# Two of eleven gate/up groups by a seven-product scheme in an fp32 feed-forward kernel

## The chip, the cores and the metric

The kernel runs on one core of a Trainium2 chip. The metric is the time of one execution on the device in microseconds; the time before is the median of three runs, 965.41 us (964.82 to 967.43). The engines of a core work side by side, each through its own list of instructions in order: PE multiplies matrices, DVE works element by element, ACT does activations and casts, POOL small things, and SP issues the DMAs. Semaphores tie them together.

## The reference

Two layers, each with a half-step feed-forward block, a mixer (attention) and a second feed-forward block, on 256 tokens of width 1024:

```
D_MODEL = 1024; SEQ = 256; DEPTH = 2; D_FF = 2816
def swiglu(h, w_gate, w_up, w_down):
    return (jax.nn.silu(h @ w_gate) * (h @ w_up)) @ w_down
...
    for i in range(DEPTH):
        h = rmsnorm(x, ffn1_norm[i])
        x = x + 0.5 * swiglu(h, ffn1_w_gate[i], ffn1_w_up[i], ffn1_w_down[i])
        ...
        h = rmsnorm(x, ffn2_norm[i])
        x = x + 0.5 * swiglu(h, ffn2_w_gate[i], ffn2_w_up[i], ffn2_w_down[i])
```

## The kernel before

All weights are fp32. A product in that precision is made of three matmuls of rounded parts: each operand is split into hi (its value rounded to PE's fp32r) and lo (what the rounding left), and PE adds x_hi·w_hi, x_hi·w_lo and x_lo·w_hi in one bank. That is `dense` (lines 416, 419 and 422): one *dense step* multiplies a 128 x 128 block of x with a 128 x 512 block of weights.

A **gate/up stage** (`gu`; there are four, one for each feed-forward block) computes h @ w_gate and h @ w_up. It takes the 2816 hidden columns in 11 groups of 256 (256 of gate and 256 of up stand side by side, 512 columns), and each group in two **chunks** of 512 rows, 1 MB each. A chunk is loaded by two DMAs, gate and up, into one of three raw buffers (line 281), split by ACT (`hi`, a cast, line 321) and DVE (`lo`, a subtraction, line 340), 512 columns at a time, into one of four hi/lo buffers, and multiplied with both halves of the tokens: 8 dense steps, 24 matmuls. Then `evac` makes h = silu(gate) * up of each token half (ACT `sil`, line 526; DVE `h`, line 529), transposes 32 x 32 blocks (line 537) and turns the rest by way of DRAM (`hd` out, `hr` back), after which h is split in its turn (`ht`, lines 557 and 559, or with small sums for some chunks, lines 573 to 586). The **down** projection follows (`acc`); there, three chunks of the last three stages are already multiplied by a seven-product scheme (`seven`, `m`).

The program writes its own order. A planner (`Flow`) keeps a clock for PE and free times for the other engines while the kernel is being recorded; generators for the loads, casts, residuals and evacuations are resumed as their estimated times come due, and each instruction is recorded in the order in which this happens. So numbers such as `yield flow.now + 4.0` (how long the read of `hr` is thought to take) move instructions and are no waits on the chip. `raw_left` and `hl_left` count the free raw and hi/lo buffers, `banks` the eight PSUM banks, `g2` and `g4` the scratch tiles. On the chip each instruction waits for semaphores, in its engine's order.

## Time and profile before

| | before |
|---|---|
| median of 3 runs | 965.41 us (964.82 to 967.43) |
| the profiled execution | 964.95 us |
| its span, first to last instruction | 963.2 us |
| granted PE clock | 1.000 |
| HBM read | 188.99 MB |

The profile is of one execution. A row of a group gives line, engine, operation, output<-inputs, shape and count, then busy time in total and the mean of one in ns, then the idle time of the engine just before. A row of a timeline gives start and length in us, and in brackets how long the engine had been idle and what ended that. In a table of stretches each engine has its busy time and count, then come the granted clock of PE, the share of the DMA engines and GB/s. PE's records overlap, because matmuls are pipelined: their distance is read from start to start.

### The profile page before, as it was taken

Reading aid. Unit: us, or ns where it says so; the run is one execution under the profiler, and the core shown is the slowest. Engines: PE = TensorE matmul, PEld = TensorE weight load, DVE = VectorE, ACT = ScalarE, POOL = GpSimd, SP = SyncE. Lnnn points to the kernel's source line nnn. Section 1 sums busy time; section 2 is a strip of 40 time slices with the busy share of each in tenths; the row PEclk is TensorE's granted clock in tenths of the full one; section 3 lists DMA queues with packets and bytes.
Section 4 is the critical chain, followed back from the end, with each engine's and each line's share of the span. In section 5 each row is a group of like instructions: output and inputs, shape, how many; then the busy total and the mean of one; then the engine's idle time right before and its main releaser. Section 6 shows DMA issues by size and latency. Waiting matters only on the chain.

```text
span 963.2 us, 13464 instructions
## 1 busy us (share of the span) xinstructions
PE 954.8 (99%) x4525; PEld 783.9 (81%) x4525; DVE 745.0 (77%) x1569; ACT 567.9 (59%) x1215; POOL 60.5 (6%) x65
## 2 busy tenths in 40 slices
PE   8999999999999999999999999999999999999998
PEld 7888888888777888888888888888787788888886
DVE  6777777788777877759986775797989886776785
ACT  6655555666676655545645555565677765554551
POOL 0000000021210000000000000000343100000000
PEclk9999999999999999999999999999999999999999
DMA  8988877486525479766568777666641468777661
GB/s 282 328 267 285 250 263 246 145 272 208 176 88 175 154 224 284 235 229 205 184 208 254 247 245 220 212 202 219 207 143 44 134 196 283 232 254 225 215 190 44
DMA packets 169295, 204.04 MB, mean 212 GB/s; under 512 B 9673, under 2 KB 144394, under 8 KB 169226
## 3 DMA queue, kind: packets, MB, share of 16 engines
q1 hardware_dynamic: 169226, 203.18, 66.0%
q8 instruction: 35, 0.57, 0.2%
q14 instruction: 34, 0.28, 0.1%
HBM read 188.99 MB, written 14.16 MB: 211 GB/s over the span
## 4 chain that ended last, share of the span: by engine, by line
PE 94%; DVE 3%; ACT 1%; DMA 1%; SPq 0%; issue 0%; ACTq 0%
PE gu L422 17%; PE gu L416 17%; PE gu L419 17%; PE acc L416 9%; PE acc L422 9%; PE acc L419 9%; PE pj L422 3%; PE pj L416 3%; PE pj L419 3%; PE xtp L429 1%; PE ptp L429 1%; PE S L1139 1%; PE AV L1220 1%; PE m L422 1%; PE m L419 1%; PE m L416 1%
## 5 line engine op out<-in xcount | busy, mean ns | idle before, releaser
L340 DVE TENSOR_TENSOR lo<-raw,hi 128x512 fp32r<-128x512 f32 x647 | 413.7, 684 | 103.9 <-ACT hi L321 100.0
L321 ACT CAST hi<-raw 128x512 fp32r<-128x512 f32 x647 | 361.7, 618 | 219.0 <-PE gu L422 123.6
L422 PE MATMUL gu<-hi,xl 128*128 128x512 f32 x704 | 274.3, 390 | 0.0
L416 PE MATMUL gu<-hi,xh 128*128 128x512 f32 x704 | 274.1, 389 | 0.0
L419 PE MATMUL gu<-lo,xh 128*128 128x512 f32 x704 | 274.0, 389 | 0.0
L422 PEld LDWEIGHTS gu<-hi,xl 128*128 128x128 f32 x704 | 132.2, 188 | 27.4
L419 PEld LDWEIGHTS gu<-lo,xh 128*128 128x128 f32 x704 | 132.2, 188 | 27.3
L416 PEld LDWEIGHTS gu<-hi,xh 128*128 128x128 f32 x704 | 132.2, 188 | 27.3
L416 PE MATMUL acc<-hi,ht 128*128 128x512 f32 x280 | 109.6, 391 | 0.0
L422 PE MATMUL acc<-hi,ht 128*128 128x512 f32 x280 | 109.2, 390 | 0.0
L419 PE MATMUL acc<-lo,ht 128*128 128x512 f32 x280 | 109.1, 390 | 0.0
L422 PE MATMUL pj<-hi,xl 128*128 128x512 f32 x160 | 64.5, 403 | 0.0
L419 PE MATMUL pj<-lo,xh 128*128 128x512 f32 x160 | 63.6, 397 | 0.0
L416 PE MATMUL pj<-hi,xh 128*128 128x512 f32 x160 | 63.5, 397 | 0.0
L422 PEld LDWEIGHTS acc<-hi,ht 128*128 128x128 f32 x280 | 52.6, 188 | 11.0
L419 PEld LDWEIGHTS acc<-lo,ht 128*128 128x128 f32 x280 | 52.6, 188 | 10.7
L416 PEld LDWEIGHTS acc<-hi,ht 128*128 128x128 f32 x280 | 52.6, 188 | 10.7
L526 ACT ACTIVATE sil<-gu,xr 128x256 f32<-128x256 f32 x88 | 41.5, 472 | 28.6 <-PE gu L422 28.6
L559 DVE TENSOR_TENSOR ht<-hr,ht 128x512 fp32r<-128x512 f32 x35 | 24.1, 687 | 32.2 <-ACT ht L557 32.2
L529 DVE SCALAR_TENSOR_TENSOR h<-gu,xr,sil 128x256 f32<-128x256 f32 x88 | 42.2, 479 | 5.8 <-ACT sil L526 4.5
L557 ACT CAST ht<-hr 128x512 fp32r<-128x512 f32 x35 | 21.6, 618 | 41.9 <-DMA hr<-hd 41.8
L436 POOL TENSOR_TENSOR xr<-v,nhalf 128x1 f32<-128x1 f32 x12 | 8.4, 698 | 502.3 <-DVE v L434 502.3
(191 smaller groups left out, 1069.0 us busy)
## 6 DMA issues: line engine op xcount, KB each, us to landing
raw<-in_ffn_w_down_dram SPq DMA_DIRECT2D x176, 256.0 KB, 4.1
raw<-in_ffn_w_gate_dram SPq DMA_DIRECT2D x86, 512.0 KB, 4.3
raw<-in_ffn_w_up_dram SPq DMA_DIRECT2D x86, 512.0 KB, 5.5
raw<-in_w_in_dram SPq DMA_DIRECT2D x32, 512.0 KB, 4.1
hd<-hb SPq DMA_DIRECT2D x44, 256.0 KB, 2.3
hr<-hd SPq DMA_DIRECT2D x44, 256.0 KB, 5.3
raw<-in_w_out_dram SPq DMA_DIRECT2D x8, 1024.0 KB, 5.0
raw<-in_w_mem_kv_dram SPq DMA_DIRECT2D x4, 1024.0 KB, 5.4
```

The source lines that it names most:

```text
L321: nc.scalar.copy(out=c.part(0, q), in_=c.block(q))
L340: nc.vector.tensor_sub(c.part(1, q), c.block(q), c.part(0, q).bitcast(F32))
L416: nc.tensor.matmul(out=ps, lhsT=xh, rhs=wh, start=start, stop=False)
L419: nc.tensor.matmul(out=ps, lhsT=xh, rhs=wl, start=False, stop=False)
L422: nc.tensor.matmul(out=ps, lhsT=xl, rhs=wh, start=False, stop=stop)
L429: nc.tensor.transpose(out=dst, in_=src, identity=flip if flipped else ident)
L526: nc.scalar.activation(sil, ps[tb][:, 0:256], AF.Silu, scale=xt.r[tb])
L529: nc.vector.scalar_tensor_tensor(out=h, in0=ps[tb][:, 256:512], scalar=xt.r[tb], in1=sil, op0=ALU.mult, op1=ALU.mult)
L557: nc.scalar.copy(out=hi, in_=src)
L559: nc.vector.tensor_sub(lo, src, hi.bitcast(F32))
L1139: nc.tensor.matmul(out=ss[e][:, pr, :nk], lhsT=q[rows, pr, :], rhs=k[rows, pr, :], start=i == 0, stop=i == len(passes) - 1)
L1220: nc.tensor.matmul(out=av[64 * e:64 * e + 64, pr, :], lhsT=vsrc(kb, pr, e), rhs=pts[e][:, pr, kb, :], start=(kb == 0), stop=(kb == nb - 1))
```

## The change

In the last three of the four gate/up stages, groups 3 and 4 are computed together. Take the normalised tokens as two halves of 128 (1 and 2) and the 1024 inputs as two halves of 512: X11, X12, X21, X22. Take the weights of both groups as B11, B21 (group 3, the two chunks) and B12, B22 (group 4). Instead of eight products of such blocks there are seven, each of four dense steps:

```
T1 = B12 - B11    T3 = B22 - B12    T2 = B22 - T1    T4 = B21 - T2
F0 = X21 + X22    F2 = X11 - X21    F1 = F0 - X11    F3 = X12 - F1
m1 = X11 B11   m5 = F0 T1   m7 = F2 T3   m6 = F1 T2   m3 = F3 B22   m2 = X12 B21   m4 = X22 T4
group 3: m1 + m2 and m1 + m6 + m7 + m4      group 4: m1 + m6 + m5 + m3 and m1 + m6 + m5 + m7
```

DVE makes the T (`wsum`, line 338 of the changed kernel) from raw weights, 512 columns at a time, and they are split as weights are. The forms F (`y`, `xf`) are made once a stage from the scaled, transposed tokens, which `prep_half` now keeps. The products go to banks of their own (`pair_m`), and DVE adds them up (`pair_sums`, line 770) into scratch tiles, from which `evac` reads. The order of work is products and plain chunks in turn: after group 2, m1, chunk, m5, chunk, m7, chunk, m6, chunk, m3, two chunks, m2, chunk, m4, and the remaining chunks; block 11 is loaded first, then 12, 22 and 21 where the list has them. Raw blocks are held until the last sum that reads them.

Besides, every chunk of gate/up weights but the first two of the program is now split 1024 columns at a time, two casts and two residuals instead of four (blocks that enter products unsummed too); summed blocks and all other weights stay at 512. And the planner counts 6.5 us instead of 4.0 for the read of `hr`.

The diff, cut to its core:

```diff
+    class Item:
+        def __init__(self, raws, uses=8, w=1):
+            self.raws, self.uses = raws, uses
+            self.hi = self.lo = None
+            self.hit, self.lot, self.st = [None] * 7, [None] * 7, [None] * 4
+            self.n, self.frees, self.takes, self.gives = 1, 1, 0, 0
+            self.sums, self.t = [], []
+            self.index = len(items)
+            w = 1 if len(items) < 2 else w
+            self.units = [(self.own(q, w), q, w, None) for q in range(0, 4, w)]
+            items.append(self)
...
+        for i, it in enumerate(items):
+            yield lambda: hl_left[0] >= it.n and all(r.raw is not None for r in it.raws)
+            hl_left[0] -= it.n
+            yield max(r.early or r.arrive for r in it.raws)
+            it.hi, it.lo = ([whl.tile([P, 2048], F32R, tag=x, name=f"{x}{i}_{j}") for j in range(it.n)]
+                            for x in ("hi", "lo"))
+            for src, q, w, dep in it.units:
                 if q == 2:
+                    yield max(r.arrive for r in it.raws)
+                if dep is not None:
+                    yield lambda: it.st[dep] is not None
+                    yield it.st[dep]
                 yield calm_a(i)
+                nc.scalar.copy(out=it.part(0, q, w), in_=src())
+                t = flow.act(512 * w)
+                it.hit[q:q + w] = [t] * w
 
     def split_lo():
+        for i, it in enumerate(items):
+            if it.sums:
+                yield lambda: all(r.raw is not None for r in it.raws) and g2.left >= it.takes + 2
+                yield max(r.arrive for r in it.raws)
+                it.t += [g2.take([P, 512], F32, "wsum") for _ in range(it.takes)]
+                for j, (x, y) in enumerate(it.sums):
                     yield calm_v(i)
+                    nc.vector.tensor_sub(it.t[j], x(), y())
+                    it.st[j] = flow.dve(512)
+            for src, q, w, dep in it.units:
+                yield lambda: it.hit[q] is not None
+                yield it.hit[q]
                 yield calm_v(i)
+                nc.vector.tensor_sub(it.part(1, q, w), src(), it.part(0, q, w).bitcast(F32))
+                t = flow.dve(512 * w)
+                it.lot[q:q + w] = [t] * w
+            raw_left[0] += it.frees
+            g2.give(it.gives)
...
+    PAIR = {(0, 1): None, (0, 2): 3, (1, 1): 3, (1, 2): 3}
...
+    def pair_items(raws):
+        r11, r12, r22, r21 = raws
+        def sums(need, x, y, held=None):
+            it = Item(need, 4)
+            it.t, it.takes = (held.t, 0) if held else ([], 4)
+            at_ = lambda v, j: it.own(j, 1, v) if isinstance(v, int) else (lambda: v.t[j])
+            it.sums = [(at_(x, j), at_(y, j)) for j in range(4)]
+            it.units = [((lambda j=j: it.t[j]), j, 1, j) for j in range(4)]
+            return it
+        def plain(r, frees):
+            it = Item([r], 4, 2)
+            it.frees = frees
+            return it
+        made = {}
+        def m1():
+            made["b11"] = plain(r11, 0)
+        def m5():
+            made["t1"] = sums([r12, r11], 0, 1)
+        def m7():
+            made["t3"] = sums([r22, r12], 0, 1)
+            made["t3"].gives = 4
+        def m6():
+            made["t2"] = sums([r22], 0, made["t1"], made["t1"])
+            made["t2"].frees = 0
+        def m3():
+            made["b22"] = plain(r22, 1)
+        def m2():
+            made["b21"] = plain(r21, 0)
+        def m4():
+            made["t4"] = sums([r21], 0, made["t2"], made["t2"])
+            made["t4"].gives = 4
+        return made, dict(m1=m1, m5=m5, m7=m7, m6=m6, m3=m3, m2=m2, m4=m4)
...
+        gu = {}
+        pair = PAIR[l, nm]
+        work = [(g, c) for g in range(NG) for c in range(2)]
+        if pair is not None:
+            rest = [w for w in work if w[0] not in (pair, pair + 1)]
+            n = 2 * pair
+            p = iter(rest[n:])
+            work = rest[:n]
+            loads = {}
+            for x in ("11", "m1", "p", "12", "m5", "p", "22", "m7", "p", "m6", "p", "m3", "p", "p", "21", "m2", "p", "m4"):
+                work.append(next(p) if x == "p" else x)
+            work += list(p)
+            blocks = {"11": (pair, 0), "12": (pair + 1, 0), "22": (pair + 1, 1), "21": (pair, 1)}
+            raws = [Chunk(parts(*blocks[x])) for x in ("11", "12", "22", "21")]
+            made, mk = pair_items(raws)
+            which = dict(zip(("11", "12", "22", "21"), raws))
+        for w in work:
+            if w in ("11", "12", "22", "21"):
+                chunks.append(which[w])
+            elif isinstance(w, str):
+                mk[w]()
+            else:
+                gu[w] = add_chunk(parts(*w), 8, 2)
...
+        if xt.keep:
+            xt.y[tb, hf] = y
+        else:
+            g2.give()
...
-                banks.give()
+                (gives or (banks, banks))[tb].give()
...
-            yield flow.now + 4.0
+            yield flow.now + 6.5
...
+        def pair_forms():
+            yield lambda: len(xt.y) == 4 and g4.left >= 4
+            y = xt.y
+            fm = [g4.take([P, 2, 4, P], F32R, "xf") for _ in range(4)]
+            for j, op, o, a, b in ((0, nc.vector.tensor_add, (1, 1), (1, 0), (1, 1)),
+                                   (2, nc.vector.tensor_sub, (1, 0), (0, 0), (1, 0)),
+                                   (1, nc.vector.tensor_sub, (0, 0), (1, 1), (0, 0)),
+                                   (3, nc.vector.tensor_sub, (0, 1), (0, 1), (0, 0))):
+                yield lambda: flow.free["V"] <= flow.now + SLACK
+                op(y[o], y[a], y[b])
+                flow.dve(512)
+            for j, o in ((0, (1, 1)), (2, (1, 0)), (1, (0, 0)), (3, (0, 1))):
+                yield lambda: flow.free["A"] <= flow.now + SLACK
+                nc.scalar.copy(out=fm[j][:, 0], in_=y[o])
+                yield flow.act(512)
+                yield lambda: flow.free["V"] <= flow.now + SLACK
+                nc.vector.tensor_sub(fm[j][:, 1], y[o], fm[j].bitcast(F32)[:, 0])
+                xt.ft[j] = flow.dve(512)
+                g2.give()
+            xt.fm = fm
+        def pair_sums():
+            def plus(o, x, m):
+                nc.vector.tensor_add(o, x, m)
+                return flow.dve(512)
+            yield lambda: "m1" in mt
+            yield mt["m1"]
+            yield g2.has()
+            u = g2.take([P, 512], F32, "gu_u")
+            nc.scalar.copy(out=u, in_=pb["m1"])
+            yield flow.act(512)
+            banks.give()
+            yield lambda: "m6" in mt and "m7" in mt
+            yield mt["m6"]
+            yield g2.has(3)
+            u2, w, v = (g2.take([P, 512], F32, "gu_v") for _ in range(3))
+            plus(u2, u, pb["m6"])
+            banks.give()
+            plus(w, u2, pb["m5"])
+            banks.give()
+            t = plus(v, w, pb["m7"])
+            pps[1][1], pend[1][1] = v, t
+            plus(u2, u2, pb["m7"])
+            banks.give()
+            for m, (g, tb), x in (("m3", (1, 0), w), ("m2", (0, 0), u), ("m4", (0, 1), u2)):
+                yield lambda: m in mt
+                yield mt[m]
+                t = plus(x, x, pb[m])
+                banks.give()
+                pps[g][tb], pend[g][tb] = x, t
+        def product(m):
+            name, left = {"m1": ("b11", (0, 0)), "m5": ("t1", 0), "m7": ("t3", 2), "m6": ("t2", 1), "m3": ("b22", 3),
+                          "m2": ("b21", (0, 1)), "m4": ("t4", (1, 1))}[m]
+            flow.until(banks.has())
+            pb[m] = bank("pair_" + m, (P, 512))
+            if m == "m1":
+                flow.spawn(pair_sums())
+                for e in range(2):
+                    flow.spawn(evac(pair + e, pps[e], pend[e], (g2, g2)))
+            for k in range(4):
+                if isinstance(left, int):
+                    flow.until(lambda: xt.ft[left] is not None)
+                    f = xt.fm[left]
+                    fh, fl, ready = f[:, 0, k, :], f[:, 1, k, :], lambda: xt.ft[left]
+                else:
+                    tb, kk = left[0], 4 * left[1] + k
+                    fh, fl, ready = xt.h[tb][:, kk, :], xt.l[tb][:, kk, :], lambda: xt.t[tb][kk]
+                t = dense(pb[m], fh, fl, ready, pit[name], k, k == 0, k == 3)
+            mt[m] = t
+            if m == "m3":
+                g4.give(4)
+        if pair is not None:
+            flow.spawn(pair_forms())
+        work = list(plan[l, nm, "work"])
+        if (l, nm) != (0, 1):
+            for tb in range(2):
+                for c in range(2):
+                    plain_chunk(0, c, (tb,))
+            work = work[2:]
+        for w in work:
+            if isinstance(w, str):
+                product(w)
+            else:
+                plain_chunk(*w, range(2))
```

How this moves instructions, at three places of the second gate/up stage. On PE, behind the first plain chunk that follows group 2 and m1 (hi58; in the program before, the same number is the second chunk of group 3). Rows of before, then of the change:

```order
L416 MATMUL gu0_3668<-hi58_0_3564,xh0_2996 128x512
L419 MATMUL gu0_3668<-lo58_0_3565,xh0_2996 128x512
L422 MATMUL gu0_3668<-hi58_0_3564,xl0_2998 128x512
L416 MATMUL gu1_3669<-hi58_0_3564,xh1_2997 128x512
L419 MATMUL gu1_3669<-lo58_0_3565,xh1_2997 128x512
L422 MATMUL gu1_3669<-hi58_0_3564,xl1_2999 128x512
```

```order
L496 MATMUL gu1_3589<-hi58_0_3461,xh1_2917 128x512
L499 MATMUL gu1_3589<-lo58_0_3462,xh1_2917 128x512
L502 MATMUL gu1_3589<-hi58_0_3461,xl1_2919 128x512
L496 MATMUL pair_m5_3645<-hi59_0_3512,xf_3328 128x512
L499 MATMUL pair_m5_3645<-lo59_0_3513,xf_3328 128x512
L502 MATMUL pair_m5_3645<-hi59_0_3512,xf_3328 128x512
```

A chunk served both token halves, each with a bank of its own; the split block hi59 (T1) now serves one product of 12 matmuls.

On DVE, the residuals in the same stage: lo60 is the plain chunk behind m5, lo61 the residual of T3 (for m7), raw61 block 22 and raw59 block 12; sf and h7 are the sums and the split of h for the down projection. Before (rows of the same numbers, plain chunks):

```order
L340 TENSOR_TENSOR lo60_0_3666<-raw60_3541,hi60_0_3665 128x512
L907 TENSOR_TENSOR ropew_1273<-ropew_1273 128x64
L340 TENSOR_TENSOR lo61_0_3725<-raw61_3606,hi61_0_3724 128x512 x4
L917 TENSOR_SCALAR ropew_1273<-ropew_1273 128x64
L529 SCALAR_TENSOR_TENSOR h_3760<-gu0_3668,xr_3002,sil_3754 128x256
```

and of the change:

```order
L344 TENSOR_TENSOR lo60_0_3561<-raw60_3486,hi60_0_3560 128x1024
L621 STREAM_TRANSPOSE hb_3548<-h_3578 128x2x4x32
L657 TENSOR_TENSOR sf_3608<-hr_3533 128x128
L657 TENSOR_TENSOR sf_3608<-sf_3608,hr_3533 128x128
L657 TENSOR_TENSOR sf_3608<-hr_3533 128x128
L657 TENSOR_TENSOR sf_3608<-hr_3533,sf_3608 128x128
L338 TENSOR_TENSOR wsum_3600<-raw61_3552,raw59_3432 128x512
L338 TENSOR_TENSOR wsum_3601<-raw61_3552,raw59_3432 128x512
L670 TENSOR_TENSOR h7_3607<-hr_3533,h7_3606 128x256
L670 TENSOR_TENSOR h7_3607<-hr_3533,h7_3606 128x128
L338 TENSOR_TENSOR wsum_3602<-raw61_3552,raw59_3432 128x512
L670 TENSOR_TENSOR h7_3607<-sf_3608,h7_3606 128x512
```

Between two weight blocks stand four subtractions, which need block 22 loaded, and only then the four residuals that PE waits for. Behind these rows follow the last subtraction, four residuals of T3, two of the chunk behind m7, four subtractions and four residuals of T2 (for m6), and between them two h, two transposes and one ht.

On SP, which issues the DMAs: loads of raw weights, with hd and hr between them. Before:

```order
L281 DMA raw60_3541<-in_ffn2_w_gate_dram 128x4x256
L281 DMA raw60_3541<-in_ffn2_w_up_dram 128x4x256
L543 DMA hd_3603<-hb_3554 128x512
L281 DMA raw61_3606<-in_ffn2_w_gate_dram 128x4x256
L281 DMA raw61_3606<-in_ffn2_w_up_dram 128x4x256
L548 DMA hr_3634<-hd_3603 128x4x128
```

and of the change:

```order
L288 DMA raw60_3486<-in_ffn2_w_gate_dram 128x4x256
L288 DMA raw60_3486<-in_ffn2_w_up_dram 128x4x256
L627 DMA hd_3507<-hb_3451 128x512
L632 DMA hr_3533<-hd_3507 128x4x128
L288 DMA raw61_3552<-in_ffn2_w_gate_dram 128x4x256
L288 DMA raw61_3552<-in_ffn2_w_up_dram 128x4x256
L288 DMA raw62_3585<-in_ffn2_w_gate_dram 128x4x256
L288 DMA raw62_3585<-in_ffn2_w_up_dram 128x4x256
```

raw61 takes the buffer of block 11 and can only be issued after T1 has been formed; raw62 takes that of raw60, and both stand behind hr, which waits for hd to land.

More of the change, by code (lines that the diff above doesn't have):

```diff
@@ L371, with seven_item @@
     WO = (0, 1, 2, 3)
[L373 to L382 removed]
+    def seven_item(it):
+        r = [it.own(q) for q in range(4)]
+        t = lambda j: lambda: it.t[j]
+        it.n, it.uses, it.takes, it.gives = 2, 7, 4, 4
+        it.sums = [(r[1], r[0]), (r[3], t(0)), (r[3], r[1]), (r[2], t(1))]
+        it.units = [(r[0], 0, 1, None), (r[2], 1, 1, None), (r[3], 2, 1, None)] + [(t(j), 3 + j, 1, j) for j in range(4)]
@@ L383, in plan_ffn @@
         plan[l, nm, "gu"] = gu
+        plan[l, nm, "work"] = [w for w in work if w not in ("11", "12", "22", "21")]
+        if pair is not None:
+            plan[l, nm, "pair"] = made
         dn = []
@@ L515, in ffn, with evac @@
         prog = [-1]
-        def evac(g, ps, end):
+        def evac(g, ps, end, gives=None):
             hb = None
@@ L638, in seven_sums, with plain_chunk @@
             g2.give(2)
-        for g, ids in enumerate(plan[l, nm, "gu"]):
-            flow.until(banks.has(2))
-            ps = [bank(f"gu{tb}", (P, 512)) for tb in range(2)]
-            end = [None, None]
-            flow.spawn(evac(g, ps, end))
-            order = [(tb, c) for tb in range(2) for c in range(2)] if g == 0 and (l, nm) != (0, 1) else \
-                    [(tb, c) for c in range(2) for tb in range(2)]
-            for tb, c in order:
+        open_ = {}
+        def plain_chunk(g, c, tbs):
+            if g not in open_:
+                flow.until(banks.has(2))
+                open_[g] = [bank(f"gu{tb}", (P, 512)) for tb in range(2)], [None, None]
+                flow.spawn(evac(g, *open_[g]))
+            ps, end = open_[g]
+            for tb in tbs:
@@ L1405 @@
     flow.step()
-    xt = Xt()
+    xt = Xt(PAIR[0, 1] is not None)
     def start_gain():
```

117 lines of the change are left out of this document (38 added, 79 removed).

## Prediction, made before the run

> **What bounds the kernel now.** I read the page first (share of each engine, then the chain that ended last), then the busy time by stretch of the program, then the waits, then the timelines of one gate/up stage.
>
> ```profile
> span 963.2 us, 13464 instructions
> PE 954.8 (99%) x4525; PEld 783.9 (81%) x4525; DVE 745.0 (77%) x1569; ACT 567.9 (59%) x1215; POOL 60.5 (6%) x65
> PE 94%; DVE 3%; ACT 1%; DMA 1%; SPq 0%; issue 0%; ACTq 0%
> core 0: us, PE busy (x) PEld busy (x) DVE busy (x) ACT busy (x) POOL busy (x), PEclk, DMA share, GB/s
> 12.40:130.60 118.20, 118.20 (x524) 97.65 (x523) 90.50 (x178) 72.02 (x150) 2.59 (x4) 1.00 0.89 283
> 316.50:437.70 121.20, 121.20 (x539) 100.30 (x538) 90.45 (x209) 68.23 (x134) 1.98 (x2) 1.00 0.72 226
> 496.00:617.10 121.10, 121.10 (x538) 100.27 (x537) 86.59 (x164) 67.44 (x132) 0.86 (x1) 1.00 0.75 235
> 782.00:901.40 119.40, 119.40 (x531) 98.89 (x530) 84.58 (x163) 66.57 (x132) 1.50 (x2) 1.00 0.73 230
> ```
>
> The chain is 94% PE, and the four stretches, one for each gate/up stage, have PE busy in every microsecond at the full granted clock. DVE is busy for 71 to 75% of the last three. So there a matmul less is time less, as long as DVE still delivers the split weights in time. A busy PE is not yet a PE at its pace, so I take the pace from two matmuls far apart in one stage:
>
> ```profile
> 867.82 0.39 PE L422 MATMUL gu<-hi,xl 128*128 128x512 f32 x1
> ...
> 879.83 0.39 PE L419 MATMUL gu<-lo,xh 128*128 128x512 f32 x1
> ```
>
> 53 starts lie between these rows: 12.01 / 53 = 0.2266 us each, nowhere a hole. A chunk of weights (8 dense steps, 24 matmuls) is 5.44 us of PE. How far the split runs ahead is in the waits and in the engines' rows at the same place:
>
> ```profile
> ACT hi L321 <- PE gu L422: 123.6, 65, 2.9
> 852.65 2.18 ACT L321 CAST hi<-raw 128x512 fp32r<-128x512 f32 x4 [1.91 <-issue]
> 874.36 2.18 ACT L321 CAST hi<-raw 128x512 fp32r<-128x512 f32 x4 [2.33 <-PE gu L422]
> 853.30 2.50 DVE L340 TENSOR_TENSOR lo<-raw,hi 128x512 fp32r<-128x512 f32 x4 [0.74 <-ACT hi L321]
> ```
>
> ACT waited 123.6 us in all for PE to give back one of the four hi/lo buffers. A cast that starts as the buffer comes free is three chunks ahead: 3 x 5.44 - 0.2 = 16.1 us. The last residual of the chunk cast at 852.65 ends at 853.30 + 2.50 = 855.80, so the split has a **lead of about 13 us** over PE. That lead, and DVE's idle quarter, are what the change spends.
>
> **The change part by part.** *PE loses work.* Two groups are 2 x 16 dense steps of three matmuls; seven products of four dense steps are 28. So 4 x 3 = 12 matmuls go from each of three stages: 36 x 0.2266 = **8.16 us** off the path. The shapes stay, so the pace does. The Trainium skill ("TensorE: Matmul & The Clock Gate", Back-to-back issue gap) gives N/2.4 + 2.5 ns between warm matmuls, 215.8 ns at 512 columns; by it the sum would be 7.8 us. The row above has 226.6 ns, and I keep the row.
>
> *DVE gets more work.* Prices are from starts that follow one another without idle:
>
> ```profile
> 563.95 0.28 DVE L573 TENSOR_TENSOR sf<-hr 128x128 f32<-128x128 f32 x1
> 564.15 0.29 DVE L573 TENSOR_TENSOR sf<-hr,sf 128x128 f32<-128x128 f32 x1
> 564.35 0.69 DVE L340 TENSOR_TENSOR lo<-raw,hi 128x512 fp32r<-128x512 f32 x1
> 564.95 0.48 DVE L529 SCALAR_TENSOR_TENSOR h<-gu,xr,sil 128x256 f32<-128x256 f32 x1
> 565.35 0.68 DVE L340 TENSOR_TENSOR lo<-raw,hi 128x512 fp32r<-128x512 f32 x1
> 565.95 0.44 DVE L537 STREAM_TRANSPOSE hb<-h 128x256 f32<-128x256 f32 x1
> 566.31 0.59 DVE L586 TENSOR_TENSOR h<-hr,h 128x256 fp32r<-128x256 f32 x2
> 566.81 0.69 DVE L340 TENSOR_TENSOR lo<-raw,hi 128x512 fp32r<-128x512 f32 x1
> ```
>
> A 512-column add or subtract takes its engine 0.60 us, a 128-column one 0.20, h 0.40, its transpose 0.36, the pair of small casts' residuals 0.50. No row shows 1024 columns. Bounds: 1.20 (two narrow ones) from above, 2 x 0.60 less one 0.07 start cost (what 0.60 holds beyond 512 columns at the slope (0.60 - 0.20) / 384) = 1.13 from below; I take 1.14, next to the slope's end. Before, a stage splits 88 quarters: 52.8 us. After: 18 plain chunks and three unsummed blocks in 42 wide residuals (47.9), and four summed blocks with four subtractions and four residuals each (32 x 0.60 = 19.2), 67.1 in all. With the eight instructions for the four token forms (4.8) and seven sums of products (4.2), a stage's DVE work rises by 14.3 + 4.8 + 4.2 = 23.3 us. In 496.00:617.10 that is 86.6 + 23.3 = 109.9 us of 121.1 - 2.7 = 118.4, 93%. On average it fits; the question is the place.
>
> The worst stretch runs from the last residual of the plain chunk behind m5 to the last residual of t2, which m6 reads (its first half stands in the second order block). Rows of that order: 18 instructions of 512 columns (10.8), two wide ones (2.3), four 128-column forms and the pair 256 + 128 (1.3), two h (0.8), three transposes (1.1): 16.3 us. PE does a chunk, m7 and a chunk meanwhile, 5.44 + 2.72 + 5.44 = 13.6. So the lead **falls by 2.7 us** there. What is it at the start? The three items ahead of that chunk are product, chunk, product, 10.9 us; less 0.2, one wide cast (at most 2 x 0.52, from 2.18 us for four) and two wide residuals with their tail, 10.9 - 0.2 - 1.0 - 2.4 = **7.2 us**. It ends at 4.5. From m6 to m3, a block that needs no sums, PE does 8.2 us and DVE 4.5, and the lead is back. Each stage's other stretches lose less. So by DVE's own work PE never waits, and this edit costs nothing; its cover is these 4.5 us a stage.
>
> *ACT.* 5 us more casts on 67 of 121: no bound. *Wide splits* save some 0.06 us a pair in all four gate/up stages, where DVE waited anyway: 0.
>
> *Raw buffers.* Blocks stay in their buffers until the sums have read them, so loads start later: block 12, the chunk behind m5, block 22 and the chunk behind m7 each wait for DVE to finish with a buffer.
>
> ```profile
> raw<-in_ffn_w_up_dram SPq DMA_DIRECT2D x86, 512.0 KB, 5.5
> hr<-hd SPq DMA_DIRECT2D x44, 256.0 KB, 5.3
> L281 SPq DMA_DIRECT2D raw<-in_ffn_w_up_dram x17: 499/501/509, 786.4 to 867.1; - x17
> DMA to landing us min/median/max: 2.9/4.6/7.8
> ```
>
> Up is issued 0.5 us behind gate, lands 5.5 later, and some 0.2 goes to hand-overs: 6.2 us. DVE's own work between the release and the first need, counted in its order at the prices above, is 6.2, 5.7, 7.2 and 6.1 us for the four (the wide cast of the two chunks taken off). So DVE stands still for 0 + 0.5 + 0 + 0.1 = 0.6 us; with the chunk behind m5 at the longest landing of the third stage, 7.8, it is 2.8 + 0.1 = 2.9. Both are under 4.5. I take no cost to PE, and keep the worse case for the range. SP's queue holds hd and hr between these loads, and a load that waits for DVE holds up what is behind it; hr is needed only for the down projection.
>
> *h rounded later.*
>
> ```profile
> ACT ht L557 <- DMA hr<-hd: 41.8, 25, 2.8
> ```
>
> The planner now counts 6.5 us for hr where it landed in 5.3; these 41.8 us of ACT's wait should mostly go, and DVE's wait for ACT behind it. ACT and DVE were ahead there, so it gains nothing by itself; it keeps waits out of the tight stretch.
>
> *Order at the third stage's start.* The last transpose of x stands two matmuls later.
>
> ```profile
> 785.98 0.60 PE L429 MATMUL xtp<-ident,x 128*128 128x128 f32 x4
> 788.82 0.68 DVE L465 TENSOR_TENSOR xl<-y,xh 128x512 fp32r<-128x512 f32 x1
> ```
>
> From it to the finished low part is 789.50 - 785.98 = 3.5 us; behind it now stand the transposes themselves (0.7) and 15 matmuls (3.4) before the first that reads that part: 4.1 us cover 3.5. Nothing is lost, and 0.6 us are left.
>
> **Sum.** The profiled execution took 964.95 us, 1.75 more than its span of 963.2. 964.95 - 8.16 = 956.8; the median of the runs, 965.41, is 0.5 above that execution, so the forecast is **957.2 us**.
>
> **The rivals.** *DVE late by part.* The 4.5 us are used up by what I left out: late loads (2.9 a stage) and hand-overs between ACT and DVE, which alternate on the summed blocks. Each microsecond beyond costs PE 3 us over the stages: 1 to 1.8 us give 960 to 962.5, 1.8 to 3.7 give 962.5 to 968, no change that can be told (within 0.3%, 2.9 us, about what a measurement of this kernel can tell). For it: 93% of DVE's time is planned. Against: in the 7 starts above DVE lost nothing between instructions of four kinds. The Trainium skill ("VectorE: DVE Perf Modes", The DRAIN you can't avoid) says that the next instruction starts only when the pipe is empty, so each would cost its full record, 0.68. By it the stretch would take 2.2 us more, and the lead would end at 2.3: still no wait, but half the cover. The rows disagree, 564.35 to 564.95, so it adds only a little to this rival's chance.
>
> *Loads in series: slower.* If the four loads land late, each late microsecond is lost in turn, since every one is released by DVE work behind the last. PE must lose 11 us, 3.7 a stage, to be slower than before by 0.3%, so DVE must lose 4.5 + 3.7 = 8.2. The covers are 25.2 us together; (25.2 + 8.2) / 4 = 8.35 us from release to need, a landing of 7.6 us. The row's median is 4.6, 7.8 its longest, so all four would have to be as slow as the slowest; and these stages move 230 GB/s where the first moved 283. If so: 968 or more.
>
> *The change doesn't do it:* the matmuls go, but PE waits at a new place, a bank say. In the order, each bank that a product takes is released by DVE ahead of that product's first residual. I fold it into the first rival.
>
> **How the numbers follow.** Forecast (955.8 to 960) 0.76; DVE late by part, still faster, 0.09; late to no change 0.09; slower 0.06. Faster 0.85, same 0.09, slower 0.06. The low end is the sum less 1.4 us, for the attention of the second layer, whose chain passes through DVE and whose order shifts:
>
> ```profile
> 685.80 1.90 DVE lo L340 x3
> 690.11 1.15 DVE lo L340
> ```
>
> The high end, 962.5, leaves out the last two cases, 0.15.
>
> **What would show it.** 608 matmuls of gu a line instead of 704 and 84 of the products, still 0.2266 us apart through the pairs; PE busy in full in three stretches some 2.7 us shorter; DVE near 85% of the span; ACT's wait for gu far below 123.6 us; no wait of PE for lo. Holes in PE before m7 or m6, with DVE waiting for raw, would prove the forecast wrong; so would a 1024-column residual above 1.2 us.

## The result, and the profile after

| | before | after |
|---|---|---|
| median of 8 runs each | 965.27 us | 960.31 us (958.92 to 963.33) |
| ratio | | 0.9945 (95%: 0.9931 to 0.996) |
| the profiled execution | 964.95 us | 962.03 us |
| its span | 963.2 us | 960.3 us |

Faster by 5.0 us between the medians (by the ratio 0.55%, 0.40 to 0.69%). That is inside the range, but 3.1 us above the forecast of 957.2 and just outside its own case, 955.8 to 960: of the 8.2 us that PE gives up, more than a third doesn't arrive. The eight runs lie in two groups, four at 958.9 to 959.5 us with a mean granted clock of 0.999 or 1.000, four at 961.1 to 963.3 with 0.998; the profile is one of the second group, and where the first loses some 2 us against the forecast no trace shows.

The page of after, its first lines and the shares of the chain that ended last:

```profile
span 960.3 us, 13252 instructions
PE 948.0 (99%) x4489; PEld 776.9 (81%) x4489; DVE 806.0 (84%) x1532; ACT 577.8 (60%) x1100; POOL 63.1 (7%) x65
PE 87%; DVE 8%; DMA 2%; ACT 1%; SPq 1%; issue 1%; DVEq 0%; ACTq 0%
```

And the stretches of the three changed stages, with the down projection behind the second of them (columns as in the table of before: busy time and count of each engine, clock, DMA share, GB/s):

```profile
318.30:435.70 117.40, 117.40 (x522) 97.24 (x520) 106.25 (x173) 71.21 (x110) 2.31 (x2) 1.00 0.73 231
495.00:612.40 117.40, 117.40 (x522) 97.24 (x521) 103.58 (x169) 66.78 (x101) 0.86 (x1) 1.00 0.74 239
612.40:660.00 47.60, 45.59 (x201) 37.14 (x199) 45.49 (x87) 33.13 (x63) 0.00 (x0) 1.00 0.65 211
780.70:898.40 117.70, 117.67 (x521) 97.14 (x520) 105.78 (x167) 70.94 (x109) 1.50 (x2) 1.00 0.73 230
```

From the first matmul of gate/up to the first of the down projection the three stages take 117.43, 117.43 and 117.72 us, where they took 120.17, 120.15 and 120.16. In these stages the change does what was counted, without a hole, and DVE is busy for 88 to 90% of them, where 93% was worked out for the second. The loss stands in the third row: PE is busy for 45.59 of 47.60 us. Between the second changed stage and the next, 164.14 us before have become 168.34. PE's timeline there (start, length, operation, and in brackets the idle time and what ended it):

```profile
656.58 0.39 PE L496 MATMUL acc<-hi,ht 128*128 128x512 f32 x1
658.13 0.50 PE L499 MATMUL acc<-lo,ht 128*128 128x512 f32 x1 [1.17 <-DVE lo L344]
...
658.71 0.39 PE L496 MATMUL acc<-hi,ht 128*128 128x512 f32 x1
659.94 0.69 PE L499 MATMUL acc<-lo,ht 128*128 128x512 f32 x1 [0.85 <-DVE lo L344]
```

And the same place in stretches, with the clock ahead of the last two columns:

```profile
657.00:660.00 3.00, 1.02 (x4) 0.55 (x4) 3.00 (x6) 2.90 (x5) 0.00 (x0) 1.00 0.92 275
660.00:663.50 3.50, 3.50 (x9) 2.73 (x10) 3.49 (x6) 0.75 (x2) 0.00 (x0) 0.51 0.73 217
663.50:667.00 3.50, 3.50 (x19) 2.90 (x18) 1.52 (x3) 1.25 (x3) 0.00 (x0) 1.00 0.99 347
```

Two steps that take 1.55 and 1.23 us from start to start instead of 0.23 are a hole of 2.3 us, and behind it PE runs for 3.4 us at a granted clock of one half: another 1.7. Both together are nearly all of the 4.2 us. The rest of the profiled run's difference is the start, 0.8 us (PE stood 3.0 us for a piece of x, where it was 0.9 before and 0.6 to 3.0 in the other runs), and 0.3 in the third stage.

Why did the last residuals of that down projection come late? Among the longest pieces of the chain that ended last (start, length, what) are two DMAs ahead of it:

```profile
603.50 5.23 DMA hd<-hb
608.79 3.98 DMA hr<-hd
```

The timelines of DVE, SP and ACT around them:

```profile
598.99 0.44 DVE L621 STREAM_TRANSPOSE hb<-h 128x256 f32<-128x256 f32 x1
600.90 2.55 SPq L288 DMA_DIRECT2D raw<-in_ffn_w_down_dram  x4
603.50 0.58 SPq L627 DMA_DIRECT2D hd<-hb  x1
605.55 0.62 ACT L641 CAST ht<-hr 128x512 fp32r<-128x512 f32 x1 [3.38 <-DMA hr<-hd]
612.80 0.62 ACT L641 CAST ht<-hr 128x512 fp32r<-128x512 f32 x1 [6.62 <-DMA hr<-hd]
613.32 0.62 ACT L326 CAST hi<-raw 128x512 fp32r<-128x512 f32 x1
613.45 0.69 DVE L643 TENSOR_TENSOR ht<-hr,ht 128x512 fp32r<-128x512 f32 x1 [3.93 <-ACT ht L641]
```

hb was ready at 599.43; hd was issued at 603.50, behind four weight loads in SP's queue; hr landed at 612.77. These 13.3 us stand against 3.0 + 6.5 = 9.5 in the planner (3.0 is its wait behind `hd`). ACT stood in front of it, in order, for 6.62 us, with the cast of the next weights behind, and DVE for 3.93. What the hr wait did in the whole kernel is in the waits:

```profile
ACT ht L641 <- DMA hr<-hd: 65.1, 22, 6.6
ACT hi L326 <- PE gu L502: 45.0, 27, 2.3
```

The wait that the third edit was to take away has grown from 41.8 to 65.1 us, and ACT's reserve, its wait for gu, has shrunk from 123.6 to 45.0. (Its wait for weights, `raw`, has grown from 7.6 to 43.4 us: the loads do come later, as the held buffers make them.) So the theory to test (**Q**): what costs time is ACT standing in its own order in front of an hr that hasn't landed. Its rival (**D**): DVE's work has used up the lead, and nothing about hr matters.

### The profile page after: what moved, and what is told of

It reads as the page before. It is cut to its first block, busy times and chain, and to the rows that moved or that the text cites. A ratio compares the mean times of both kernels' runs of the same rounds, so it can differ in the third digit from the quotient of the medians.

```text
span 960.3 us, 13252 instructions
## 1 busy us (share of the span) xinstructions
PE 948.0 (99%) x4489; PEld 776.9 (81%) x4489; DVE 806.0 (84%) x1532; ACT 577.8 (60%) x1100; POOL 63.1 (7%) x65
## 4 chain that ended last, share of the span: by engine, by line
PE 87%; DVE 8%; DMA 2%; ACT 1%; SPq 1%; issue 1%; DVEq 0%; ACTq 0%
PE gu L502 14%; PE gu L499 14%; PE gu L496 14%; PE acc L496 8%; PE acc L502 8%; PE acc L499 8%; DVE lo L344 3%; PE pj L502 3%; PE pj L499 3%; PE pj L496 3%; PE pair_m L502 2%; PE pair_m L499 2%; PE pair_m L496 2%; PE xtp L509 1%; PE S L1320 1%; PE AV L1401 1%
## 5 line engine op out<-in xcount | busy, mean ns | idle before, releaser
L326 ACT CAST hi<-raw 128x512 fp32r<-128x512 f32 (+1 forms) x469 | 338.2, 771 | 160.9 <-DMA raw<-in_ffn_w_up_dram 43.4
L344 DVE TENSOR_TENSOR lo<-raw,hi 128x512 fp32r<-128x512 f32 (+1 forms) x469 | 393.0, 873 | 45.4 <-ACT hi L326 44.6
L502 PE MATMUL gu<-hi,xl 128*128 128x512 f32 x608 | 236.9, 390 | 0.0
L496 PE MATMUL gu<-hi,xh 128*128 128x512 f32 x608 | 236.8, 389 | 0.0
L499 PE MATMUL gu<-lo,xh 128*128 128x512 f32 x608 | 236.7, 389 | 0.0
L502 PEld LDWEIGHTS gu<-hi,xl 128*128 128x128 f32 x608 | 114.1, 188 | 23.7
L499 PEld LDWEIGHTS gu<-lo,xh 128*128 128x128 f32 x608 | 114.1, 188 | 23.6
L496 PEld LDWEIGHTS gu<-hi,xh 128*128 128x128 f32 x608 | 114.2, 188 | 23.5
L641 ACT CAST ht<-hr 128x512 fp32r<-128x512 f32 x35 | 21.7, 619 | 65.2 <-DMA hr<-hd 65.1
L326 ACT CAST hi<-wsum 128x512 fp32r<-128x512 f32 x84 | 49.2, 621 | 15.7 <-DVE wsum L338 12.3
L344 DVE TENSOR_TENSOR lo<-wsum,hi 128x512 fp32r<-128x512 f32 x84 | 53.0, 682 | 0.0
```

Source lines behind the costliest of these rows:

```text
L326: nc.scalar.copy(out=it.part(0, q, w), in_=src())
L344: nc.vector.tensor_sub(it.part(1, q, w), src(), it.part(0, q, w).bitcast(F32))
L496: nc.tensor.matmul(out=ps, lhsT=xh, rhs=wh, start=start, stop=False)
L499: nc.tensor.matmul(out=ps, lhsT=xh, rhs=wl, start=False, stop=False)
L502: nc.tensor.matmul(out=ps, lhsT=xl, rhs=wh, start=False, stop=stop)
L641: nc.scalar.copy(out=hi, in_=src)
```

## The experiments

All are edits of the changed kernel; the times of before ran along on the same chip (965.1 to 965.3 us). Where a ratio is given it is to those.

**hd and hr off SP's queue.** On PE, DVE and ACT the order of instructions is the same.

```diff
-            nc.sync.dma_start(out=hd...
+            nc.gpsimd.dma_start(out=hd...
-            nc.sync.dma_start(out=hr, in_=hd...
+            nc.gpsimd.dma_start(out=hr, in_=hd...
```

> The changed kernel with the two small transfers of h (hd out, hr back) issued by POOL instead of SP; the order on PE, DVE and ACT is the same instruction for instruction. In the profiled run PE stood 2.6 us near 658 us (end of the third feed-forward's down projection), and its clock read 0.52 and 0.63 in the four microseconds behind. Theory Q (queue): ACT stood 3.4 + 6.6 us for hr just before, because hd and hr wait in SP's queue behind weight loads and hold those up in turn; off that queue hr comes earlier. Then ACT's wait for hr falls from 65 to under 40 us, the lead at the first seven-product item of that down projection rises from 1.3 to over 4 us, the hole goes and the time is 956 to 957.8. Theory D (DVE's own work): the pair used the lead up and DVE, 95% busy there, cannot win it back; the time stays 959 to 961 whatever the queue. Rival: POOL issues more slowly than SP, hr comes later, ACT's wait grows and the time is above 961.

957.27 us, ratio 0.9916 (0.9901 to 0.9931); span 955.1, the span before less 8.1. The timeline of this run, with the same cast on ACT, the residuals behind it on DVE and PE's first use of them:

```profile
608.78 0.62 ACT L641 CAST ht<-hr 128x512 fp32r<-128x512 f32 x1 [5.22 <-DMA hr<-hd]
610.25 1.89 DVE L344 TENSOR_TENSOR lo<-raw,hi 128x512 fp32r<-128x512 f32 x3
617.04 0.39 PE L499 MATMUL m<-lo,h 128*128 128x512 f32 x1
```

The same residuals and matmul in after:

```profile
614.26 1.89 DVE L344 TENSOR_TENSOR lo<-raw,hi 128x512 fp32r<-128x512 f32 x3
618.04 0.39 PE L499 MATMUL m<-lo,h 128*128 128x512 f32 x1
```

And the stretch of the down projection in this run:

```profile
611.40:659.00 47.60, 47.60 (x212) 39.37 (x211) 46.63 (x88) 31.58 (x60) 1.31 (x2) 1.00 0.69 223
```

From the start of these residuals to the matmul it is 6.8 us here and 3.8 in after: 3 us more lead (from the end of the fourth residual, 4.3 against 1.3), and PE is busy for all of the projection. Q's time and lead came, D's did not; but the total wait for hr hardly fell (61.0 us, expected under 40). So it isn't the sum of the wait that costs, but where it falls: here the one wait in a place with little lead. This edit also takes hd and hr out of the way of the weight loads, so it doesn't tell by itself which of the two helped; the run with 10 us below, with SP's queue as it was, does.

**The third edit undone**, on SP's queue and on POOL's.

```diff
-            yield flow.now + 6.5
+            yield flow.now + 4.0
```

> The changed kernel with the third edit undone: hr is counted 4.0 us after its issue again, so ACT's cast of h and the residual behind it stand earlier in their queues. My prediction gave this edit 0 us: then 959 to 961. Theory Q: the cast then stands still longer in front of the weights' casts; ACT's wait for hr goes from 65 to 85 us or more, the hole grows by 1 to 4 us: 961 to 965. Theory D: the wait moves, DVE's sum of work does not: 959 to 961.

963.83 us, ratio 0.9985 (0.9973 to 0.9996). The edit to which the prediction gave 0 is worth 3.5 us. Without it 1.5 us of the gain are left. ACT's wait for hr:

```profile
ACT ht L641 <- DMA hr<-hd: 105.8, 29, 9.3
```

And PE's timeline at the end of the first changed stage's down projection, where after has no hole:

```profile
482.28 0.50 PE L499 MATMUL acc<-lo,ht 128*128 128x512 f32 x1 [0.77 <-DVE lo L344]
484.81 0.50 PE L499 MATMUL acc<-lo,ht 128*128 128x512 f32 x1 [1.55 <-DVE lo L344]
```

The loss sits elsewhere than in after: 5.0 us between the first changed stage and the next, and 1.1 where after lost 4.2.

> hd and hr issued by POOL, and hr counted 4.0 us after its issue. Tells the queue from the place in ACT's order. From hd's data to hr landed takes some 10 to 13 us in the traces against 7 planned here (3.0 + 4.0) and 9.5 with 6.5. If the place in ACT's order is what counts, POOL's queue gives back only some 3 us a wait: ACT's wait for hr 85 to 105 us, holes as in the run with 4.0 us on SP but smaller, 958.5 to 962. If SP's queue alone did it: 956.8 to 958.

969.47 us, ratio 1.004 (1.002 to 1.0061), from 965.38 to 974.31: above both ranges, and ACT's wait for hr, 111.7 us, is above what was expected too. So POOL's queue alone doesn't cure: with the earlier place in ACT's order the wait is back. Why this is even slower than on SP stays open; the profiled run is the fastest of the ten.

**The other way: a later place, hd and hr on SP.**

```diff
-            yield flow.now + 6.5
+            yield flow.now + 10.0
```

> The changed kernel (hd and hr on SP) with hr counted 10 us after its issue instead of 6.5: the cast of h and its residual stand later in the queues of ACT and DVE. Theory Q, as the last runs left it (off SP's queue hr came 2.9 us earlier, the lead at the first seven-product item rose from 1.3 to 4.3 us and the hole went): what costs time is ACT standing in order in front of an hr that hasn't landed, so a later place does what an earlier hr does: ACT's wait for hr under 45 us, no hole at the end of the down projections, 956.5 to 958. Rival L (late forms): the last groups' forms of h come too late for the down projection or keep their buffers too long, PE waits for ht or a split waits for a buffer: 959 to 963.

957.78 us (957.02 to 962.43, four runs), ratio 0.9925 (0.99 to 0.9949). This interval still overlaps that of the changed kernel (0.9931 to 0.996), so that the gain of 2.5 us rests on the trace as well as on the times. The wait for hr is nearly gone:

```profile
ACT ht L641 <- DMA hr<-hd: 13.5, 4, 6.6
```

And in the same down projection PE is busy throughout:

```profile
611.90:659.50 47.60, 47.60 (x211) 39.38 (x210) 43.87 (x84) 29.54 (x55) 0.00 (x0) 1.00 0.71 222
```

Q again. With both cures:

> Both cures together: hd and hr issued by POOL and hr counted 10 us after its issue. Either alone left PE without a hole (spans of 955.1 and 955.5 us in the profiled runs, which is the span before, 963.2, less 8.1). Theory Q: there is nothing left to gain, the sum of PE's work is the bound: 956.8 to 957.8, and fewer of the runs 2 us above the others. If the later place and POOL's queue together bring the forms of h too late for the down projection: 959 to 963.

958.19 us, ratio 0.9926 (0.9913 to 0.9939), span of the profiled run 955.7: nothing further, as Q has it. That fewer of the runs would lie above the others did not come true: three of six took 958.9 to 960.2 us, the others 956.7 to 957.5. There is no trace of those three, and what they lose is open.

**Without the pair** in the stage ahead of the hole, and without any (`PAIR` None for it, or for all).

> The changed kernel with the pair left out of the second of its three stages (495 to 612 us), the one ahead of the hole. Both theories: that stage is 2.7 us longer, the lead at its end stays near 13 us, the hole and the low clock behind it (together 4.2 us) go: 960.3 - 4.2 + 2.7 = 958.8 for a run that had both, near 960 for one that had a smaller hole; so 958.5 to 960.3. If the hole has nothing to do with that pair (a late transfer, the order of the down projection), it stays and the time is 962 to 963.5.

959.76 us, ratio 0.9934 (0.9922 to 0.9946): a kernel with 12 matmuls more is no slower than the changed one. The hole is gone, as both theories had it, although ACT waited 70.9 us for hr in this run.

> The changed kernel without any pair: what is left of the change is the 1024-column split in the four gate/up stages and the 6.5 us for hr. My prediction: both worth 0, so 964.8 to 966. Theory Q allows a gain where the kernel before had its last weights just in time (lead 1.3 us first, -1.1 us last in two down projections) without a hole: still 964.8 to 966, but with ACT's wait for hr under 41.8 us. If the wide split delays PE's first reads, or the later rounding delays the down projection, slower: 967 or more.

965.63 us, ratio 1.0002 (0.999 to 1.0013). ACT waited 69.5 us for hr, more than before (expected under 41.8, a miss), and it cost nothing: the lead at the same first seven-product item, measured as above, is 9.5 us here instead of 1.3, and no wait of ACT reaches PE. Without the pair the later place and the wide splits together are worth nothing; with it the later place is worth 3.5 us.

**DVE's work, more and less.** All splits 512 wide (`w` 1 in place of 2 for the chunks and the blocks), with 6.5 us, then with 10.

> The changed kernel with every split 512 columns wide; pair and 6.5 us stay, hd and hr on SP. My prediction gave the wide splits 0 by themselves. By the rows a pair of narrow residuals is 1.20 and a wide one about 1.13, so a stage's DVE work grows by 42 x 0.07 = 2.9 us. If the lead at the entry of the down projections falls by some of that, the just-in-time ends there (lead -0.3 to -3.9 us for the last residual) turn into longer holes: 961 to 965, ACT's wait for gu under 45 us. If the finer grain makes up for it (a cast and a residual hand over in halves): 959 to 961.

959.04 us, ratio 0.9929 (0.9912 to 0.9945): not slower, whatever 42 more instructions a stage cost DVE. That ACT's reserve fell came true (its wait for gu 21.2 us), the price did not. ACT's wait for hr fell as well, to 47.3 us, so this run changes more than DVE's work.

> The kernel with hr counted 10 us after its issue, and every split 512 columns wide: some 2.9 us more work for DVE in each gate/up stage (42 x 0.07), ACT's order without the waits for hr. Theory Q: DVE's own work costs nothing as long as nobody stands for hr; the time is that of hr_10us, 956.8 to 958. Theory D: DVE is the bound behind it all, and 2.9 us more a stage show: 960 to 966.

959.83 us, ratio 0.9943 (0.9927 to 0.9959), between the two theories. In its profile the first changed stage's down projection has a hole of its own:

```profile
479.84 0.39 PE L496 MATMUL acc<-hi,ht 128*128 128x512 f32 x1
481.48 0.50 PE L499 MATMUL acc<-lo,ht 128*128 128x512 f32 x1 [1.25 <-DVE lo L344]
```

The intervals of all four kernels with 6.5 or 10 us on SP and either width overlap; what the widths are worth by themselves is below what these runs tell. At the last chunk of a down projection the margin is about nothing (in before, too, the last chunk's residuals ended only as they were needed), so small shifts make or close a hole of 1 to 2 us there.

**The pair's sums of weights on POOL**, 16 a stage, with 10 us for hr.

```diff
+                    if it.n == 1:
+                        nc.gpsimd.tensor_sub(it.t[j], x(), y())
+                        it.st[j] = flow.pool(1.9)
```

> The kernel with hr counted 10 us after its issue, and the pair's sums and differences of weights (16 a stage) made by POOL instead of DVE: 9.6 us less for DVE in each stage. From POOL's row for 128x256, 0.954 us, I estimate 1.9 us for 512 columns. Theory Q: PE waits for nothing in hr_10us, so DVE's relief gains nothing: 956.8 to 958. Theory D: gains, 955 to 956.5. Rival P: POOL is so slow, or gets so much in DVE's way, that the products' weights come late: four sums in a row take 7.6 us where a product's lead was 3 to 6 us; 959 to 970.

982.06 us, ratio 1.0168 (1.0151 to 1.0185): the rival P, and more than it gave. Groups by line and shape in this run, the sums' two and two of DVE (busy time, mean ns of one, then the idle time before):

```profile
L339 POOL TENSOR_TENSOR wsum<-raw,wsum 128x512 f32<-128x512 f32 x24 | 44.7, 1892 | 69.3 <-DMA raw<-in_ffn_w_up_dram 48.5 <-DVE lo L348 20.8
L339 POOL TENSOR_TENSOR wsum<-raw,raw 128x512 f32<-128x512 f32 x24 | 35.6, 1515 | 75.4 <-DMA raw<-in_ffn_w_up_dram 75.4
L348 DVE TENSOR_TENSOR lo<-wsum,hi 128x512 fp32r<-128x512 f32 x84 | 61.8, 768 | 11.9 <-ACT hi L326 11.3
L647 DVE TENSOR_TENSOR ht<-hr,ht 128x512 fp32r<-128x512 f32 x35 | 28.2, 807 | 0.2
```

The two groups of DVE in the run with 10 us and the sums on DVE:

```profile
L344 DVE TENSOR_TENSOR lo<-wsum,hi 128x512 fp32r<-128x512 f32 x84 | 53.3, 681 | 0.0
L643 DVE TENSOR_TENSOR ht<-hr,ht 128x512 fp32r<-128x512 f32 x35 | 24.0, 685 | 3.0 <-ACT ht L641 3.0
```

A sum takes 1.5 to 1.9 us instead of 0.60, a load is freed that much later, PE stood for lo 14.0 us in front of plain chunks and 3.2 in front of products, the clock fell to one half twice, and some of DVE's instructions got slower beside POOL.

**A fourth pair**, in the first stage (groups 5 and 6), first with hd and hr on POOL.

```diff
-    PAIR = {(0, 1): None, (0, 2): 3, (1, 1): 3, (1, 2): 3}
+    PAIR = {(0, 1): 5, (0, 2): 3, (1, 1): 3, (1, 2): 3}
...
-        yield g2.has(8)
+        yield lambda: len(memd) == 4 and g2.left >= 8
```

> hd and hr on POOL, and a pair in the first gate/up stage too (its groups 5 and 6; the preparation of mem waits until its four pieces are there). A fourth pair takes another 12 x 0.2266 = 2.7 us from PE: 954.6 if the split's lead holds there (12 to 14 us in the second half of that stage, before) and mem's forms are ready for its products; 955 to 960 if mem's forms come late or the stage, whose weights take 0.9 of the DMA engines' time, runs into its transfers; above 960 if PE stands in front of the products of mem for several microseconds.

962.42 us, ratio 0.997 (0.9957 to 0.9983). The stage gives 2.0 of its 2.7 us (119.12 from its first matmul to the down projection, against 121.12 in the run on POOL without it and 121.2 to 121.8 in the others), but PE stands in front of the products of mem, as its timeline has it:

```profile
198.01 0.50 PE L502 MATMUL kv<-hi,meml 128*128 128x512 f32 x1 [1.55 <-DVE meml L970]
```

And in the stretches there the clock drops again:

```profile
193.00:200.00 7.00, 3.70 (x15) 1.95 (x14) 6.74 (x18) 4.89 (x12) 0.55 (x1) 0.97 0.77 251
200.00:203.50 3.50, 3.50 (x10) 2.74 (x11) 3.46 (x15) 1.67 (x4) 0.00 (x0) 0.58 0.93 255
```

Then with hr at 10 us on SP, and mem's transposes let in earlier (`flow.free["V"] <= flow.now + 2.0`):

> The kernel with hr counted 10 us after its issue and a fourth pair in the first gate/up stage (groups 5 and 6); the transposes of mem may be placed while DVE has up to 2 us planned, so that mem's forms no longer wait for the pair to end. In the run before with four pairs the first stage went from 121.6 to 119.1 us, as counted, and 7.6 us were lost in front of mem's products. If that was mem's late forms: 954.6 now, no holes between 186 and 215 us. If the stage's own load on DVE makes everything behind it late: holes in the first down projection or at mem's products stay, 956 to 962.

962.78 us, ratio 0.997 (0.9954 to 0.9987). The holes in front of mem's products are gone, so they were mem's late forms; but the stage now takes 122.65 us (two steps of PE in it, at 83 and 124 us, take 2.3 and 0.9), and its down projection has a hole of its own (a step of 2.0 at 135 us). In neither order did that stage have room for a pair.

**The version to keep** is the changed kernel with either cure: 957.3 to 957.8 us, 7.5 to 8 us below before.

## Why the prediction was right, and where it was not

- *The time:* 960.31 lies 0.3 us outside the forecast's own case (955.8 to 960, chance 0.76) and in that of the rival "DVE late by part" (0.09). The way it went was forecast for the right reason, PE's lost work; that the loss stayed inside the range is luck in part: the range took in that rival, while the wait that made the loss stands in the prediction at 0.
- *PE loses work, 8.16 us:* right. 36 matmuls fewer, the pace held, the stages 2.7 us shorter each (the third 2.4), and with the hole cured the whole span is 8.1 us shorter.
- *DVE's work and the tight stretch:* right for the stretch that was worked out. In the stage of the hole the lead goes from 538.94 (gu, PE) less 532.66 (its residuals' end) = 6.3 us to 552.54 less 549.24 = 3.3 in front of m6, where 7.2 and 4.5 were worked out; the fall is 3.0 for 2.7. PE never waited there. The timeline of after, DVE and PE:

```profile
531.48 1.18 DVE L344 TENSOR_TENSOR lo<-raw,hi 128x1024 fp32r<-128x1024 f32 x1
538.94 0.39 PE L496 MATMUL gu<-hi,xh 128*128 128x512 f32 x1
546.78 2.46 DVE L344 TENSOR_TENSOR lo<-wsum,hi 128x512 fp32r<-128x512 f32 x4
552.54 0.39 PE L496 MATMUL pair_m<-hi,xf 128*128 128x512 f32 x1
578.38 0.65 DVE L344 TENSOR_TENSOR lo<-wsum,hi 128x512 fp32r<-128x512 f32 x1
582.46 0.39 PE L496 MATMUL pair_m<-hi,xh 128*128 128x512 f32 x1
599.35 1.18 DVE L344 TENSOR_TENSOR lo<-raw,hi 128x1024 fp32r<-128x1024 f32 x1
606.94 0.39 PE L496 MATMUL gu<-hi,xh 128*128 128x512 f32 x1
```

  A 1024-column residual came to 1.11 us from 531.48 to the next start, 532.59, a little under its lower bound of 1.13. The Trainium skill ("VectorE: DVE Perf Modes", The DRAIN you can't avoid), which the prediction held against these prices, also says that an instruction that is not held starts earlier; that agrees with the rows.
- *"Each stage's other stretches lose less":* wrong. The lead was back in front of m3, some 7 us, as said, but from there to m4 DVE was busy for 22.5 of 25.3 us while PE needed 21.8: in the last four rows above, the lead is 582.46 less 579.03 = 3.4 us in front of m4 and 606.94 less 600.53 = 6.4 at the stage's last chunk. In the run without any pair that chunk has 12.3 (611.58 less 599.30).
- *Its cover ends with the stage:* the prediction followed the lead from m5 to m3 and not into the down projection, where DVE is busy for 43.6 of 47.6 us before (45.5 after) and can win little back.
- *"h rounded later", 0:* the step that failed, in two ways. 6.5 us was held against hr's own 5.3 us of landing, when what counts is the way from hb through hd to hr: 13.3 us in the place that mattered, 9.5 planned, 7.0 before. So the wait did not go. And "ACT and DVE were ahead there, so it gains nothing by itself" holds for the kernel without the pair (no change); with the lead at 3 to 6 us such a wait can reach DVE, and then PE. Undoing the edit costs 3.5 us; going on to 10 gains 2.5 by the medians, with the hole gone from the trace.
- *"hr is needed only for the down projection":* PE needs it only then, but ACT's cast of it stands ahead of weights' casts, and that is where the wait hit. The text named SP's queue and stopped one engine short.
- *The rival "DVE late by part"* has the time, 960 to 962.5, and its kind, DVE late for PE, but not the place or the cause: it took 1 to 1.8 us in each of three stages for late loads and for hand-overs on the summed blocks, and the trace has 4.2 us in one down projection, behind one wait for hr. "No wait of PE for lo", a sign of the forecast, failed there (2.0 us, two waits); DVE near 85% of the span (84) and ACT's shorter wait for gu came true. Loads in series, the slower case, didn't come: ACT waited longer for loads, but PE was busy all through the stages.
- *The third stage's start, 0:* 0.3 us. The four transposes of x now stand inside a dense step and not between two; with the matmuls beside them they take 1.14 us from start to start (785.75 to 786.89) where it was 0.90.
- *The half clock* behind the hole, 1.7 us in the profiled run, was in no term.

## What to carry to other kernels

When an edit spends the lead of a producer, recheck every wait that the lead had made free, above all loads whose use stands in the order of the engine that produces: in these runs such waits cost nothing with 9.5 us of lead and up to 4.2 us with 1.3. Follow the lead past the end of the changed stage, to the next place where it can grow again. And a delay that a planner counts has to be held against the whole way on the chip, queue and both transfers, not against the last transfer.

## What the runs showed of the hardware

- *Half clock behind a cluster of small holes.* In all 14 traces the granted clock changes only at whole multiples of 3.413 us from the time at which it first is full, as if it were set window by window. In after the first window starts at 4.71 us; 192 windows later, at 660.07, the clock drops to one half, and one window later it is back. Short of the program's end it drops in four places: in after, in the run with four pairs on POOL and twice in the run with the sums on POOL. In the window ahead of each, PE's records are busy for 0.41, 0.38, 0.28 and 0.44 of the time; in every other window short of the end, for 0.48 or more. In the first two no single wait was longer than 1.6 us. So what counted here is how much of one window was idle, and thus how the holes lay to the windows. Below are the window ahead of the drop in after, and two windows of the run with 4.0 us on POOL, where a like cluster of holes lies across both (0.60 and 0.75 busy) and no drop followed:

```profile
656.66:660.07 3.41, 1.40 (x6) 0.62 (x5) 3.38 (x7) 3.29 (x6) 0.00 (x0) 1.00 0.89 270
658.79:662.20 3.41, 2.04 (x9) 1.41 (x8) 3.38 (x6) 3.10 (x6) 0.00 (x0) 1.00 0.84 250
662.20:665.62 3.42, 2.58 (x11) 1.80 (x10) 3.42 (x7) 2.18 (x4) 0.00 (x0) 1.00 0.83 253
```

  The Trainium skill ("TensorE: Matmul & The Clock Gate", What's actually happening) has the clock halve after an idle window of about 3.4 us that runs freely and isn't set by the kernel's start. The windows of 3.413 us agree; that a window counts as idle with PE busy for up to 0.44 of it goes further than the page says.
- *DVE slower beside POOL.* With the sums on POOL, DVE's subtractions of two tiles in SBUF went from 681 to 768 and from 685 to 807 ns in the mean, while the transpose hb went from 438 to 437 and h, which reads a bank, from 479 to 475. The 512-column residuals of weights that no sum enters, which lie outside the pairs, stayed at 685 ns (686). The mean hides how it comes: 31 of the 35 ht took 0.69 us at most, as before, and four, each beside a sum on POOL, 1.78, as this row of DVE's timeline (POOL's sums run there from 529.92 to 536.23):

```profile
533.30 1.78 DVE L647 TENSOR_TENSOR ht<-hr,ht 128x512 fp32r<-128x512 f32 x1
```

  The Trainium skill ("GPSIMD Engine Reference", 1. Specifications) names contention with DVE instructions that have two SBUF inputs; these rows agree and give it a size here.
